# Layer-norm scales asked for by GpSimd, and six chunks instead of five in the seven-product form in the first feed-forward of a tuned decoder trunk

## The chip, the core and the metric

The kernel runs on one core of one Trainium2 chip. Its engines run side by side and are tied together by semaphores: TensorE (PE in the profile, its weight loads PEld), VectorE (DVE), ScalarE (ACT), GpSimd (POOL) and SyncE (SP), which issues transfers. Each engine works through its own list of instructions strictly in order. The metric is device time in microseconds (us).

## The reference: what is computed

Two layers over 256 tokens of width 1024, all in float32. Each layer is a half-step feed-forward, a mixer (forgetting attention in the first layer, latent attention in the second), a second half-step feed-forward and a gated input embedding, each followed by a layer norm:

```python
def swiglu(x, w_in, w_out):
    h = x @ w_in
    gate, up = h[..., :D_FF], h[..., D_FF:]          # D_FF = 2816
    return (jax.nn.silu(gate) * up) @ w_out
...
for i in range(DEPTH):                               # DEPTH = 2
    x = post_norm(x, 0.5 * swiglu(x, ffn1_w_in[i], ffn1_w_out[i]), ln_g[i, 0], ln_b[i, 0])
    mix = fox_mixer(...) if i < N_A else mla_mixer(...)
    x = post_norm(x, mix, ln_g[i, 1], ln_b[i, 1])
    x = post_norm(x, 0.5 * swiglu(x, ffn2_w_in[i], ffn2_w_out[i]), ln_g[i, 2], ln_b[i, 2])
    gate = jax.nn.sigmoid(x @ ple_w_gate[i] + ple_b_gate[i])
    x = post_norm(x, gate * (p[i] @ ple_w_proj[i]), ln_g[i, 3], ln_b[i, 3])
```

`post_norm` is a layer norm of `ALPHA * x + delta` with a scale `g` and a shift `b` of 1024 numbers; there are eight of them.

## The kernel before

**Split products.** Every float32 operand of a matmul is split into a rounded high half and a low half (the rest), and a product is made of three matmuls: high x high, high x low, low x high (`mm3`). Weights come by DMA into one of three buffers `raw` of 1 MB; a unit of 1024 columns is split by an ACT copy (the high half, line 246, or line 254 when it is done ahead) and a DVE subtraction (the low half, line 247 or 258) into one of ten slots `hl` (plus lent tiles such as `gb`, `qk`, `ota`, `otb`). In `mm3` with a weight as the moving operand, the second of the three matmuls is the first to read the weight's low half.

**The feed-forward.** The hidden width of 2816 is cut into eleven chunks of 256. For each chunk, gate and up are 96 matmuls of 256 columns (`HT`), 48 for each half; ACT takes the silu of the gate when the first half is done (line 820), DVE multiplies it with up when the second half is done (line 826). The second product (256 hidden x 1024 out, for two token tiles) is done in one of two ways:

- *plain* (`W`): eight block products of 512 columns, 24 matmuls; two weight units.
- *seven products* (`sums`): a two-by-two block scheme with seven products instead of eight, 21 matmuls. It needs sums of blocks: three DVE additions on the weights (`add` of the stream, lines 294, 300, 302, into the tile `ts` and back into `raw`), three and a half weight units (`ws`, in the order 1, 0, 2, 3; unit 3 is half as wide) and three DVE instructions on the activations (lines 841, 845, 846), after which 896 columns of activations are split (ACT line 623, DVE line 627) into a home tile `fs`, `qk`, `ota` or `otb`.

The seven accumulators stay in PSUM over all such chunks. In the first feed-forward (`cold`) chunk 0 is computed while the first transfers land; chunks 0, 1, 2 and 8, 9, 10 are plain, chunks 3 to 7 use seven products. PE's order there is: chunk 0, then gate and up of chunks 1 to 4, the sums of chunks 3 and 4, gate and up of 5 to 7, the sums of 5 to 7, gate and up of 8 to 10, then the plain products. In the other three feed-forwards chunks 0 to 7 use seven products.

**What sets the order.** While the program is built, a planner (`Stream`) keeps estimated clocks for PE, ACT, DVE and the transfers. After each `mm3` its `pump` may emit one split or one weight addition, if a slot is free and the clocks say that DVE and ACT have caught up with PE. The result is a fixed list for each engine. Weight transfers stand in SP's list in the order of use, and each waits until the `raw` buffer that it overwrites has been split.

**Scale and shift.** `load_gb` asks for the scale and the shift of the next layer norm, 512 KB each when spread over the 128 partitions, into the one tile `gb`, with two requests in SP's list. `gb` has other users: it is lent as a weight slot in the feed-forwards, and holds the attention's decay masks. The request therefore waits until the last of these readers is done. The layer norm itself is four DVE instructions for each token tile at line 702, with a GpSimd power at line 694 ahead of the second; the first at line 702 reads the scale, the second the shift.

Of the kernel before, what the change touches and what calls it, by code (L numbers as in the profile page):

```python
# [11 lines left out]
F32R = mybir.dt.float32r  # L12
# [3 lines left out]
D = 1024  # L16
# [113 lines left out]
class Recorder:  # L130
    def __init__(self):
        self.seq = []
# [12 lines left out]
class Stream:  # L145


    def __init__(self, nc, raw_pool, pool, loads, seq):
        self.nc, self.raw_pool, self.pool, self.loads = nc, raw_pool, pool, loads
        seen = []  # L150
        self.groups = []
        for key in seq:
            g = group_of(key)
            if g not in seen:
                seen.append(g)
                self.groups.append(g)
        members = {g: [] for g in self.groups}
        self.left = {}
        for key in seq:
            if key not in self.left:  # L160
                self.left[key] = 0
                members[group_of(key)].append(key)
            self.left[key] += 1
        self.order = [k for g in self.groups for k in members[g]]
        self.index = {k: i for i, k in enumerate(self.order)}
        self.last_of = {members[g][-1]: i for i, g in enumerate(self.groups)}
        self.raw, self.hl, self.sums, self.added = {}, {}, {}, {}
        self.slots = [f"hl{i}" for i in range(NSLOT)]
        self.slot_of = {}
        self.kept = set()  # L170
        self.loaded = self.ready = 0
        self.done = 0
        self.pending = None
        self.pe_t = self.act_t = self.dve_t = self.dma_t = 0.0
        self.arrives = {}
        self.between = {}
        self.hold = False
        self.rest = None
        self.at = 0
        self.stop = None  # L180
        self.fixed = 80
        self.side = False

    def load(self, n=NRAW):
        while self.loaded < len(self.groups) and self.loaded < self.done + n:
# [81 lines left out]
        self.split_done(key, w)  # L267

    def aside(self, key):
        return self.side and key[0] == "ws" and key[-1] == 3  # L270

    def free(self):
        return self.slots or self.aside(self.order[self.ready])
# [134 lines left out]
def group_of(key):  # L408
    k = key[0]
    if k in ("win", "wiu", "fv", "kd", "dq"):  # L410
        return key[:-1] + (key[-1] // 2,)
    if k == "ws":
        return key[:-1]
    if k in ("wout", "fvb", "fvc", "fk", "fq", "fo", "pg", "pp", "mo", "qr"):
        return key[:-1] + (key[-1] // 2,)
    if k in ("kvk", "qn"):
        return ("kq", key[-1])
    return key
# [81 lines left out]
def pbcast(row, n):  # L500

    return bass.AP(tensor=row.tensor, offset=row.offset, ap=[[0, 128], [1, n]])


class Trunk:
# [162 lines left out]
    def load_gb(self, li, i):  # L668
        first = (li, i) == (0, 0)
        if first:  # L670
            self.tl([128, 16], F32, "gap0", 1)
        self.gb = self.tl([128, 2, D], F32, "gb", 1)
        if first:
            self.tl([128, 16], F32, "gap1", 1)
        if not self.rec:
            self.dma(self.gb[:, 0, :], pbcast(self.a["ln_g"][li, i], D))
            self.dma(self.gb[:, 1, :], pbcast(self.a["ln_b"][li, i], D))

    def ln_stats(self, st, t, c0, w, y, alpha):

# [37 lines left out]
    def ffn(self, li, which, lni, kv=False, ple=False, at=None, cold=False, after=()):  # L718


        nc, S = self.nc, self.S
# [1 line left out]
        g, gT, forms = {}, {}, {}  # L723
        homes = HOMES
        S.reclaim(*(homes if cold else homes[:2]))
        S.fixed, S.side = 150, not cold
        early = (0, 1, 2) if cold else ()
        plain = early + tuple(range(NCH - STAG, NCH))
        summed = [c for c in range(NCH - STAG) if c not in early]

# [5 lines left out]
        def first():  # L736
# [35 lines left out]
            gt = self.room(0, summed)  # L772
            nc.scalar.activation(gt, ps[0], AF.Silu)
            close(0, gt, ps[1])

        def act(c, t, ps):
# [27 lines left out]
        def HT(c, gate, up, what=None):  # L804
            for half in range(2):
                ps = self.bank(*(up if half else gate))
                for u in range(2):
                    w = self.use(("wiu", li, which, c, 2 * half + u))
                    for kk, b in ((kk, b) for kk in range(4) for b in range(2)):
                        k = 4 * u + kk  # L810
                        if (half, k, b) == (0, 1, 0) and what:
                            what(self.bank(*up))
                        col = slice(256 * kk + 128 * b, 256 * kk + 128 * b + 128)
                        self.mm3(
                            ps[:, 256 * b : 256 * b + 256], lambda i: w[:, i, col], lambda i: self.xT[:, :, i, k, :],
                            (k, b) == (0, 0), (k, b) == (7, 1),
                        )
                if half == 0:
                    gt = self.room(c, summed)
                    nc.scalar.activation(gt, ps, AF.Silu)  # L820
                    S.busy(act=512)
            close(c, gt, ps)

        def close(c, gt, up):
            S.ahead()
            nc.vector.tensor_tensor(gt, gt, up, op=ALU.mult)
            self.S.busy(dve=512)
            if c in summed:
                add(c)
                return  # L830
            o = self.tl([128, 2, 512], F32R, "g4", 6)
            self.high(o[:, 0, :], gt)
            S.later()
            self.low(o[:, 0, :], o[:, 1, :], gt)
            gT[c] = o

        def add(c):

            tt, f = nc.vector.tensor_tensor, self.full[c]
            b = lambda i, n=1: f[:, 128 * i : 128 * (i + n)]  # L840
            tt(
                b(4, 2).rearrange("p (a b) -> p a b", b=128), b(0)[:, None, :].to_broadcast([128, 2, 128]),
                b(1, 2).rearrange("p (a b) -> p a b", b=128), op=ALU.subtract,
            )
            tt(b(6), b(5), b(1), op=ALU.subtract)
            tt(b(7), b(6), b(3), op=ALU.add)
            S.busy(dve=700)
            tag, o = self.home(homes)
            self.high(o[:, 0, :], f[:, 128:1024])
            S.between_sums()  # L850
            self.low(o[:, 0, :], o[:, 1, :], f[:, 128:1024])
            forms[c] = tag, o
# [1077 lines left out]
```

## Time and profile before

| | us |
|---|---|
| median of 3 runs | 1055.88 (1055.67 to 1058.72) |
| the profiled execution's own time | 1054.48 |
| its span, first to last instruction | 1052.7 |
| PE busy in the span | 1037.3 (99%) |
| DVE busy | 895.0 (85%) |
| ACT busy | 592.5 (56%) |
| GpSimd busy | 59.9 (6%) |

In a timeline row the numbers are the start (us from the span's start), the time from the first start to the last end of the merged instructions, the engine, the line, the operation, output<-input by tile names, and xcount; in brackets stands the idle time of the engine just before and what ended it. Consecutive instructions overlap a little at their ends, so what an instruction costs in a row of them is the step from start to start. A row of the waits reads: waiting engine and tile <- what ended the wait: total us, times, longest. A row of the windows gives a stretch, its length, and for each engine busy us and instructions.

### The profile page before, as it was taken

The numbers are of one execution on the slowest core, as the hardware profiler recorded it, in microseconds if no ns is written. First come the engines' busy times: TensorE is split into PE (matmuls) and PEld (weight loads), VectorE is DVE, ScalarE is ACT, GpSimd is POOL, SyncE is SP. The second block draws the span as 40 slices with busy tenths as digits, with TensorE's granted clock in tenths as the row PEclk, the third lists the DMA queues.
The fourth block names the chain that finished last, engine by engine and source line by source line (L and its number), as shares of the span: only waits on it lengthen the run. The fifth ranks groups of instructions, "written<-read, shape, count | busy, mean of one in ns | idle before, by whom it ended". The sixth has DMA issues, their size and how long they took to land.

```text
span 1052.7 us, 17554 instructions
## 1 busy us (share of the span) xinstructions
PE 1037.3 (99%) x7085; PEld 949.7 (90%) x7085; DVE 895.0 (85%) x1312; ACT 592.5 (56%) x901; POOL 59.9 (6%) x88
## 2 busy tenths in 40 slices
PE   9999999999999999999899999999999999999996
PEld 8999898999889999998799898988899889898986
DVE  5788976868898979978979899898887989899877
ACT  6565563667745554663465646546776564646541
POOL 0000000123300000000220000000000000000000
PEclk9999999999999999999999999999999999999999
DMA  7855586444736374673564555742444564554732
GB/s 280 307 186 188 194 287 242 161 144 159 257 126 240 120 249 144 219 301 140 190 234 157 201 195 168 277 154 105 151 155 170 184 213 156 184 213 174 279 121 81
DMA packets 37477, 202.74 MB, mean 193 GB/s; under 512 B 3970, under 2 KB 9874, under 8 KB 16532
## 3 DMA queue, kind: packets, MB, share of 16 engines
q1 hardware_dynamic: 37396, 201.63, 54.0%
q8 instruction: 55, 0.90, 0.3%
q14 instruction: 26, 0.21, 0.1%
HBM read 200.55 MB, written 1.06 MB: 192 GB/s over the span
## 4 chain that ended last, share of the span: by engine, by line
PE 68%; DVE 3%; ACT 1%; issue 1%; POOL 0%; DVEq 0%; ACTq 0%; POOLq 0%
PE h L610 37%; PE y L610 21%; PE tr L610 8%; PE tr L614 2%; DVE hl L247 1%; DVE x L702 0%; PE h L614 0%; DVE x L683 0%; DVE st L684 0%; DVE g L1076 0%; ACT hl L246 0%; POOL rs L694 0%; DVE tr L1715 0%; ACT qk L623 0%; ACT P L1340 0%
## 5 line engine op out<-in xcount | busy, mean ns | idle before, releaser
L610 PE MATMUL h<-xT,hl 128*128 128x256 f32 x3144 | 366.9, 278 | 0.2 <-DVE hl L323 0.2
L610 PEld LDWEIGHTS h<-xT,hl 128*128 128x128 f32 x3144 | 362.8, 189 | 2.0 <-ACT xT L623 0.6
L247 DVE TENSOR_TENSOR hl<-raw,hl 128x1024 fp32r<-128x1024 f32 (+4 forms) x273 | 317.3, 1191 | 38.8 <-ACT hl L246 37.6
L246 ACT ACTIVATE hl<-raw 128x1024 fp32r<-128x1024 f32 (+4 forms) x273 | 270.0, 1027 | 72.0 <-DVE raw L302 41.0
L610 PE MATMUL y<-hl,g 128*128 128x512 f32 x336 | 78.6, 391 | 0.0
L610 PEld LDWEIGHTS y<-hl,g 128*128 128x128 f32 x336 | 62.6, 188 | 12.6
L610 PE MATMUL h<-hl,xT 128*128 128x512 f32 (+2 forms) x312 | 68.0, 371 | 0.0
L610 PEld LDWEIGHTS h<-hl,xT 128*128 128x128 f32 x312 | 54.9, 188 | 9.8
L610 PE MATMUL y<-hl,otb 128*128 128x512 f32 x219 | 58.0, 399 | 0.0
L610 PE MATMUL y<-hl,xT 128*128 128x512 f32 (+3 forms) x282 | 52.7, 334 | 0.0
L623 ACT ACTIVATE xT<-tr 128x512 fp32r<-128x512 f32 x28 | 16.3, 597 | 61.7 <-PE tr L614 61.6
L258 DVE TENSOR_TENSOR hl<-raw,hl 128x1024 fp32r<-128x1024 f32 (+2 forms) x42 | 49.7, 1188 | 1.3 <-ACT hl L254 1.2
L254 ACT ACTIVATE hl<-raw 128x1024 fp32r<-128x1024 f32 (+2 forms) x42 | 43.0, 1028 | 9.7 <-DVE raw L302 9.2
L610 PEld LDWEIGHTS y<-hl,xT 128*128 128x128 f32 x282 | 44.1, 188 | 4.6 <-ACT xT L623 0.4
L610 PEld LDWEIGHTS y<-hl,otb 128*128 128x128 f32 x219 | 39.8, 188 | 8.3 <-DVE otb L627 0.3
L610 PE MATMUL y<-hl,ota 128*128 128x512 f32 x177 | 46.7, 398 | 0.1
L694 POOL TENSOR_TENSOR rs<-ve,mhalf 128x1 f32<-128x1 f32 x16 | 15.1, 944 | 522.2 <-DVE ve L693 522.2
L610 PE MATMUL tr<-xT,hl 128*128 128x256 f32 x360 | 42.8, 278 | 0.0
L610 PEld LDWEIGHTS tr<-xT,hl 128*128 128x128 f32 x360 | 42.1, 188 | 0.3
L610 PEld LDWEIGHTS y<-hl,ota 128*128 128x128 f32 x177 | 32.8, 189 | 7.7 <-DVE hl L247 0.6
L820 ACT ACTIVATE P<-h 128x512 f32<-128x512 f32 x33 | 19.7, 596 | 33.2 <-PE h L610 32.8
L294 DVE TENSOR_TENSOR ts<-raw 128x1024 f32<-128x1024 f32 x29 | 35.4, 1222 | 0.6
(324 smaller groups left out, 1638.5 us busy)
## 6 DMA issues: line engine op xcount, KB each, us to landing
raw<-in_ffn_in_dram SPq DMA_DIRECT2D x85, 1024.0 KB, 4.9
raw<-in_ffn_out_dram SPq DMA_DIRECT2D x44, 1024.0 KB, 5.0
raw<-in_pg_dram SPq DMA_DIRECT2D x8, 1024.0 KB, 4.8
raw<-in_mo_dram SPq DMA_DIRECT2D x8, 1024.0 KB, 4.8
raw<-in_kq_dram SPq DMA_DIRECT2D x8, 640.0 KB, 4.2
gb<-in_ln_g_dram SPq DMA_DIRECT2D x8, 512.0 KB, 6.2
gb<-in_ln_b_dram SPq DMA_DIRECT2D x8, 512.0 KB, 7.6
raw<-in_fk_dram SPq DMA_DIRECT2D x4, 1024.0 KB, 5.0
```

The lines of the kernel that those rows point to most:

```text
L246: nc.scalar.activation(hi, src, AF.Copy)
L247: nc.vector.tensor_tensor(lo, src, hi.bitcast(F32), op=ALU.subtract)
L254: nc.scalar.activation(hi, src, AF.Copy)
L258: nc.vector.tensor_tensor(lo, src, hi.bitcast(F32), op=ALU.subtract)
L294: tt(s[:, 0:1024].rearrange("p (a b) -> p a b", b=512), r[:, 0:512][:, None, :].to_broadcast([128, 2, 512]), r[:, 512:1536].rearrange("p ( ...
L610: self.nc.tensor.matmul(out, lhsT, rhs, start=start, stop=stop)
L614: self.nc.tensor.transpose(out, in_, self.ident)
L623: self.nc.scalar.activation(hi, src, AF.Copy)
L694: nc.gpsimd.tensor_tensor(rs, ve, self.mhalf, op=ALU.pow)
L820: nc.scalar.activation(gt, ps, AF.Silu)
```

## The change

1. `load_gb` issues its two requests from GpSimd instead of from SP.
2. In the first feed-forward chunk 2 moves from the plain to the seven-product form: chunks 0, 1, 8, 9, 10 are plain, 2 to 7 use seven products. The sums of chunks 2, 3 and 4 now stand together, ahead of gate and up of chunk 5.
3. There, unit 3 of the weights of chunks 2 to 6 goes into the six-buffer tile `g4` instead of an `hl` slot (`aside`), as it did already in the other feed-forwards for all chunks.
4. The split activations of chunk 0 stay in the tile `PT` instead of a `g4` buffer until the plain products at the end.

```diff
-        self.side = False
+        self.side = ()
...
     def aside(self, key):
-        return self.side and key[0] == "ws" and key[-1] == 3
+        return key[0] == "ws" and key[-1] == 3 and key[-2] in self.side
...
         if not self.rec:
-            self.dma(self.gb[:, 0, :], pbcast(self.a["ln_g"][li, i], D))
-            self.dma(self.gb[:, 1, :], pbcast(self.a["ln_b"][li, i], D))
+            for k, name in enumerate(("ln_g", "ln_b")):
+                self.nc.gpsimd.dma_start(self.gb[:, k, :], pbcast(self.a[name][li, i], D))
...
-        S.fixed, S.side = 150, not cold
-        early = (0, 1, 2) if cold else ()
+        S.fixed, S.side = 150, range(2, 7) if cold else range(8)
+        early = (0, 1) if cold else ()
...
-            o = self.tl([128, 2, 512], F32R, "g4", 6)
+            o = self.tl([128, 2, 512], F32R, "PT", 1) if cold and c == 0 else self.tl([128, 2, 512], F32R, "g4", 6)
```

The planner's lists change with it in the first feed-forward and up to the middle of the first layer's attention; from there on the lists of PE, ACT and DVE are the same but for tile numbers.

DVE at the end of the first sums, before (the activations and weights of chunk 4; `hl7` and `gb` are the first weights of chunk 5's gate):

```order
L627 TENSOR_TENSOR qk_777<-P_708,qk_777 128x896
L247 TENSOR_TENSOR hl5_806<-ts_734,hl5_806 128x1024
L247 TENSOR_TENSOR hl6_815<-ts_734,hl6_815 128x512
L247 TENSOR_TENSOR hl7_823<-raw_604,hl7_823 128x1024
L881 SCALAR_TENSOR_TENSOR x0_69<-x0_69,h0_787 128x512
L247 TENSOR_TENSOR gb_836<-raw_604,gb_836 128x1024
```

DVE at the same place now (`ota_780` the activations of chunk 4, `hl4_809` and `g4_818` the last weights of chunk 3, `raw_607` the weights of chunk 4, `gb_881` the first weight of chunk 5's gate):

```order
L627 TENSOR_TENSOR ota_780<-P_711,ota_780 128x896
L247 TENSOR_TENSOR hl4_809<-ts_737,hl4_809 128x1024
L247 TENSOR_TENSOR g4_818<-ts_737,g4_818 128x512
L294 TENSOR_TENSOR ts_826<-raw_607 128x1024
L300 TENSOR_TENSOR ts_826<-ts_826,raw_607 128x512
L302 TENSOR_TENSOR raw_607<-ts_826,raw_607 128x512
L247 TENSOR_TENSOR hl5_842<-raw_607,hl5_842 128x1024
L247 TENSOR_TENSOR hl6_851<-raw_607,hl6_851 128x1024
L247 TENSOR_TENSOR hl7_860<-ts_826,hl7_860 128x1024
L881 SCALAR_TENSOR_TENSOR x0_69<-x0_69,h0_790 128x512
L247 TENSOR_TENSOR g4_873<-ts_826,g4_873 128x512
L247 TENSOR_TENSOR gb_881<-raw_729,gb_881 128x1024
```

The three weight additions and four low halves of chunk 4 now stand behind those of chunk 3; before, the next gate's weights stood there.

DVE between the two sums, before (`hl4` to `hl7` are the weights of chunk 7's gate and up, `raw_953` the summed weights of chunk 5, `P_1043` the activations of chunk 6):

```order
L247 TENSOR_TENSOR hl6_1034<-raw_906,hl6_1034 128x1024
L247 TENSOR_TENSOR hl7_1052<-raw_906,hl7_1052 128x1024
L294 TENSOR_TENSOR ts_1081<-raw_953 128x1024
L300 TENSOR_TENSOR ts_1081<-ts_1081,raw_953 128x512
L302 TENSOR_TENSOR raw_953<-ts_1081,raw_953 128x512
L247 TENSOR_TENSOR gb_1097<-raw_953,gb_1097 128x1024
L826 TENSOR_TENSOR P_1043<-P_1043,h0_1045 128x512
L841 TENSOR_TENSOR P_1043<-P_1043 128x256
L845 TENSOR_TENSOR P_1043<-P_1043 128x128
L846 TENSOR_TENSOR P_1043<-P_1043 128x128
L258 TENSOR_TENSOR hl8_1106<-raw_953,hl8_1106 128x1024
L627 TENSOR_TENSOR qk_1112<-P_1043,qk_1112 128x896
```

DVE at the same place now (`gb_1118` the last weight of chunk 7's up, `P_1077` the activations of chunk 6, `raw_1022` and `raw_1086` the weights of chunks 5 and 6):

```order
L826 TENSOR_TENSOR P_1077<-P_1077,h0_1079 128x512
L841 TENSOR_TENSOR P_1077<-P_1077 128x256
L845 TENSOR_TENSOR P_1077<-P_1077 128x128
L846 TENSOR_TENSOR P_1077<-P_1077 128x128
L627 TENSOR_TENSOR qk_1145<-P_1077,qk_1145 128x896
L294 TENSOR_TENSOR ts_1167<-raw_1022 128x1024
L300 TENSOR_TENSOR ts_1167<-ts_1167,raw_1022 128x512
L302 TENSOR_TENSOR raw_1022<-ts_1167,raw_1022 128x512
L247 TENSOR_TENSOR hl8_1192<-raw_1022,hl8_1192 128x1024
L247 TENSOR_TENSOR hl9_1210<-raw_1022,hl9_1210 128x1024
L247 TENSOR_TENSOR hl0_1225<-ts_1167,hl0_1225 128x1024
L247 TENSOR_TENSOR g4_1237<-ts_1167,g4_1237 128x512
```

The additions on chunk 5's weights and its first low halves stood ahead of chunk 6's activations, and now stand behind them. Next in the list are the three additions for chunk 6 and line 826 for chunk 7, and then (`P_1204` the activations of chunk 7, `hl1` to `g4` the weights of chunk 6, `raw_1121` the weights of chunk 7, `hl4` the first that its sums read):

```order
L841 TENSOR_TENSOR P_1204<-P_1204 128x256
L845 TENSOR_TENSOR P_1204<-P_1204 128x128
L846 TENSOR_TENSOR P_1204<-P_1204 128x128
L258 TENSOR_TENSOR hl1_1270<-raw_1086,hl1_1270 128x1024
L627 TENSOR_TENSOR ota_1276<-P_1204,ota_1276 128x896
L247 TENSOR_TENSOR hl2_1302<-raw_1086,hl2_1302 128x1024
L247 TENSOR_TENSOR hl3_1311<-ts_1248,hl3_1311 128x1024
L247 TENSOR_TENSOR g4_1320<-ts_1248,g4_1320 128x512
L294 TENSOR_TENSOR ts_1328<-raw_1121 128x1024
L300 TENSOR_TENSOR ts_1328<-ts_1328,raw_1121 128x512
L302 TENSOR_TENSOR raw_1121<-ts_1328,raw_1121 128x512
L247 TENSOR_TENSOR hl4_1338<-raw_1121,hl4_1338 128x1024
```

Before, two low halves of chunk 6 stood ahead of the activations of chunk 7, and now none does.

GpSimd's list from the layer norm behind the first layer's attention to the one behind its input embedding (- before, + now; `hl` at line 250 is the bias row of the embedding's gate):

```order
 L694 TENSOR_TENSOR rs<-ve,mhalf 128x1 x2
-L250 MEMSET hl_5077 128x1024
-L694 TENSOR_TENSOR rs<-ve,mhalf 128x1 x4
+L677 DMA gb<-in_ln_g_dram 128x1024
+L677 DMA gb<-in_ln_b_dram 128x1024
+L250 MEMSET hl_5087 128x1024
+L694 TENSOR_TENSOR rs<-ve,mhalf 128x1 x2
+L677 DMA gb<-in_ln_g_dram 128x1024
+L677 DMA gb<-in_ln_b_dram 128x1024
+L694 TENSOR_TENSOR rs<-ve,mhalf 128x1 x2
 L1444 TENSOR_TENSOR rs<-ve,mhalf 128x1
```

Each pair of requests now stands in GpSimd's list ahead of the powers of the layer norm that it serves, and is gone from SP's, where weight transfers stood behind it.

## The prediction

> **What bounds the kernel now.** I read the page's busy times first, then the waits of PE, then windows over the first feed-forward, where the change moves work.
>
> ```profile
> PE 1037.3 (99%) x7085; PEld 949.7 (90%) x7085; DVE 895.0 (85%) x1312; ACT 592.5 (56%) x901; POOL 59.9 (6%) x88
> PE h L610 <- DVE otb L247: 3.0, 1, 3.0
> PE tr L614 <- DVE x L702: 0.7, 1, 0.7
> 47.00:75.50 28.50, 28.50 (x212) 26.85 (x211) 28.12 (x33) 15.82 (x18) 0.00 (x0) 1.00 0.53 188
> 86.40:131.00 44.60, 44.47 (x328) 41.53 (x328) 43.53 (x52) 24.96 (x29) 0.00 (x0) 1.00 0.52 180
> 130.00:152.00 22.00, 22.00 (x197) 22.00 (x196) 16.18 (x17) 11.95 (x14) 0.00 (x0) 1.00 0.87 305
> ```
>
> PE sets the time: 1037.3 of 1052.7 us, and its longest named wait is 3.0 us. So a change is worth the PE work that it saves, less the waits that it makes. The three windows (length, then PE, PEld, DVE, ACT, POOL, clock) show the catch: from 47 to 75.5 and from 86.4 to 131 DVE is as full as PE, 28.12 of 28.50 and 43.53 of 44.60 us. These are the stretches around the two groups of seven-product sums. What is added to DVE there, or put in another order, reaches PE at once. From 130 to 152 (plain products) DVE idles 5.82 us.
>
> **The PE work saved.**
>
> ```profile
> 66.24 1.52 PE L610 MATMUL y<-hl,qk 128*128 128x512 f32 x6
> 68.28 0.84 PE L610 MATMUL y<-hl,qk 128*128 128x512 f32 x3
> 68.96 0.84 PE L610 MATMUL tr<-hl,qk 128*128 128x512 f32 x3
> 71.00 0.87 PE L610 MATMUL h<-xT,hl 128*128 128x256 f32 x6
> ```
>
> Three matmuls of 512 columns step 68.96 - 68.28 = 0.68 us. A chunk's sums last 71.00 - 66.24 = 4.76 us for 21, eight such threes in the plain form 8 x 0.68 = 5.44. Chunk 2 in the new form saves **0.68 us**, and that is all that this change can save on PE.
>
> **The added DVE work of chunk 2.** It adds three weight additions and one and a half units, and longer activations.
>
> ```profile
> 42.25 2.36 DVE L247 TENSOR_TENSOR hl<-raw,hl 128x1024 fp32r<-128x1024 f32 x2 [0.26 <-ACT hl L246]
> 46.99 1.23 DVE L247 TENSOR_TENSOR gb<-raw,gb 128x1024 fp32r<-128x1024 f32 x1 [2.38 <-ACT gb L246]
> 68.01 1.22 DVE L247 TENSOR_TENSOR hl<-raw,hl 128x1024 fp32r<-128x1024 f32 x1
> 70.88 4.62 DVE L247 TENSOR_TENSOR hl<-raw,hl 128x1024 fp32r<-128x1024 f32 x4
> 83.28 0.42 DVE L841 TENSOR_TENSOR P<-P 128x256 f32<-128x256 f32 x1
> 90.93 1.22 DVE L294 TENSOR_TENSOR ts<-raw 128x1024 f32<-128x1024 f32 x1
> 110.33 1.22 DVE L294 TENSOR_TENSOR ts<-raw 128x1024 f32<-128x1024 f32 x1
> 112.92 2.51 DVE L247 TENSOR_TENSOR hl<-raw,hl 128x1024 fp32r<-128x1024 f32 x2
> ```
>
> The activations (lines 841, 845, 846: about 1.1 us from the row of 0.42 and two half as wide, and a split wider by 0.4) fall into the idle 2.38 us ahead of 46.99: free. If that cover were gone they would cost their 1.5 us. From 46.99 on the list is the old one, one chunk earlier in meaning, up to the last weights of chunk 3, whose half unit ends at 68.01. There chunk 4's additions now stand where the weights of the next gate stood. Three additions last 112.92 - 110.33 = 2.59 us from the first to the first low half, so that low half runs from 70.60 to 70.60 + 1.22 = 71.82. PE comes to chunk 4 at 71.00 and reads the low half with its second matmul, one third of 0.68 later: 71.23. A wait of about **0.6 us** (0.65 with the 0.06 between a DVE end and the PE start behind it). The other low halves follow at 1.14 each against 1.36 for two products, and hold. PE is then 4.76 + 0.65 = 5.41 us late at the next gate; the sums of three chunks stand together, which is that work moved ahead, not added.
>
> **The second sums: where the price lies.** PE does gate and up of chunks 5, 6, 7, then their three sums. DVE must in the same time do the next weights, the additions and the sums' splits, and it has no spare time (the second window). What saved it before was a lead: the additions on chunk 5's weights at 90.93 stood 104.12 - 90.93 = 13.2 us ahead of its sums (row below). In the new list they stand behind line 826 and line 627 of chunk 6, as the third pair of the order lists shows. I follow DVE from A, the end of chunk 6's up on PE.
>
> ```profile
> 77.12 0.60 ACT L820 ACTIVATE P<-h 128x512 f32<-128x512 f32 x1 [4.76 <-PE h L610]
> 82.56 0.69 DVE L826 TENSOR_TENSOR P<-P,h 128x512 f32<-128x512 f32 x1 [1.50 <-PE h L610]
> 85.38 1.09 DVE L627 TENSOR_TENSOR fs<-P,fs 128x896 fp32r<-128x896 f32 x1 [1.02 <-ACT fs L623]
> 104.12 1.54 PE L610 MATMUL y<-gb,fs 128*128 128x512 f32 x6
> 105.77 0.68 DVE L826 TENSOR_TENSOR P<-P,h 128x512 f32<-128x512 f32 x1
> 107.47 1.22 DVE L258 TENSOR_TENSOR hl<-ts,hl 128x1024 fp32r<-128x1024 f32 x1
> 108.61 1.08 DVE L627 TENSOR_TENSOR ota<-P,ota 128x896 fp32r<-128x896 f32 x1
> 109.61 0.68 DVE L247 TENSOR_TENSOR hl<-ts,hl 128x512 fp32r<-128x512 f32 x1
> 113.66 1.97 PE L610 MATMUL y<-hl,ota 128*128 128x512 f32 x6
> 118.95 0.87 PE L610 MATMUL h<-xT,hl 128*128 128x256 f32 x6
> ```
>
> Line 826 cannot run before A: it waits for PE (82.56, 0.20 behind the end of chunk 5's up, as I place it from chunk 7's end at 104.12 less two chunks of 10.88, 96 matmuls at half of 0.2267). Line 627 follows at +2.82 (85.38 - 82.56, with the wait for ACT in it), that is A + 3.02. Steps from the rows: line 627 takes 1.00, a low half 1.14 (107.47 to 108.61), a half-wide one 0.72 (109.61 to 110.33), the additions 2.59, line 826 with 841 to 846 takes 1.70 (105.77 to 107.47). Then
>
> - chunk 5's additions from A + 4.02, first low half A + 6.61, three of these and the half one to A + 10.75;
> - chunk 6's additions to A + 13.34, chunk 7's line 826 and the next three to A + 15.04;
> - one low half of chunk 6 to A + 16.18, line 627 of chunk 7 to A + 17.18, two low halves and the half one to A + 20.18;
> - chunk 7's additions to A + 22.77, its first low half ends at A + 23.99.
>
> PE wants that low half at A + 10.88 (gate and up of 7) + 9.54 (113.66 - 104.12, two chunks of sums) + 0.23 = A + 20.65. With the 0.06 it waits **3.4 us** in all, in pieces at chunks 6 and 7, since A + 16.18 is already late for chunk 6 by about half a us. Before, the same third chunk took 118.95 - 113.66 = 5.29 instead of 4.76, a loss of 0.53 that goes with it.
>
> What bounds this term: below, 0.5 us, if DVE arrives at the sums as it does now; above, 3.4 plus one low half of 1.14 if ACT's high halves, which stand in its list behind line 820 (77.12, idle 4.76 for PE), come late once more. I take 3.4, since the list fixes the order and each step is a row of this stretch. What is late next: the plain weights of chunks 8 to 10 and the removed chunk 2; there the third window has DVE idle by a quarter, and the two units of chunk 2 are gone. So PE loses nothing more.
>
> **The requests on GpSimd.**
>
> ```profile
> SPq L541 <- DVE x L702: 46.5, 5, 22.4
> ACT hl L246 <- DMA raw<-in_ffn_in_dram: 7.5, 7, 2.8
> 492.77 0.33 SPq L541 DMA_DIRECT2D gb<-in_ln_g_dram  x1
> gb<-in_ln_g_dram SPq DMA_DIRECT2D x1, 512.0 KB, 3.6
> gb<-in_ln_b_dram SPq DMA_DIRECT2D x1, 512.0 KB, 9.4
> 504.58 0.75 DVE L702 SCALAR_TENSOR_TENSOR x<-x,rs,gb 128x512 f32<-128x512 f32 x1 [0.45 <-POOL rs L694]
> 506.93 0.63 PE L614 MATMUL tr<-ident,x 128*128 128x128 f32 x4 [0.71 <-DVE x L702]
> 521.65 2.03 POOL L1459 TENSOR_SCALAR PT<-PT,rs 128x256 f32<-128x256 f32 x1
> 1028.57 0.33 SPq L541 DMA_DIRECT2D gb<-in_ln_g_dram  x1
> 1038.07 0.75 DVE L702 SCALAR_TENSOR_TENSOR x<-x,rs,gb 128x512 f32<-128x512 f32 x1 [0.44 <-POOL rs L694]
> ```
>
> SP is freed of five waits, 46.5 us in all. I price this at nothing: the one larger wait for the weights of a feed-forward is ACT's 7.5 us in seven pieces, and ACT is busy 56% and splits ahead of PE, which has no wait of its own behind it. What it costs if GpSimd is slower: each request waits for the same last reader as before, so it cannot go out earlier. The trace has no transfer asked for by GpSimd; a request lies between SP's 0.33 us and the slowest GpSimd row, 2.03; I take the nearer, SP's. Two layer norms are close: behind the first input embedding the pair goes out from 492.77 and the shift is read at 504.58; at the end 1028.57 against 1038.07. Landings go from 3.6 us (the window at 492) to 9.4 (a layer norm at 987). At SP's price both hold: 0.
>
> **Sum.** -0.68 + 0.65 + 3.42 - 0.53 = **+2.9 us** on the profiled 1054.48, or 1057.35. The median of the runs lies 1055.88 - 1054.48 = 1.40 above it, so 1057.35 + 1.40 = **1058.8 us**. Items 3 and 4 of the change give slots and take no instruction away: nothing, beyond what the lists above already hold.
>
> **Rivals.** *DVE keeps up.* If the additions for chunk 5 start as far ahead as now, only -0.68 + 0.65 stays: 1055.9, and 1055.2 without either wait. For it: DVE stood idle 1.50 and 1.02 us in this stretch before (82.56, 85.38), which a late PE could fill. Against it: the list puts the additions behind line 826 of chunk 6, and that cannot move. *SP's freedom pays.* If the 3.0 us wait for `otb` at 517.8 hung on a late transfer behind the requests, it would go: 1058.8 - 3.0 = 1055.8, with the first rival 1052.2. Against it:
>
> ```profile
> 514.77 1.04 ACT L246 ACTIVATE otb<-raw 128x1024 fp32r<-128x1024 f32 x1
> 519.93 1.22 DVE L247 TENSOR_TENSOR otb<-raw,otb 128x1024 fp32r<-128x1024 f32 x1
> ```
>
> ACT had split the high half by 515.8, so the data were there; the low half stands behind DVE's layer norm, whose order does not change. *The scale and shift land late (slower).* With 2.03 us for each of two requests and 9.4 to land, the shift is there at 492.77 + 4.06 + 9.4 = 506.2, 1.6 after it is read, and PE's transposes wait directly (506.93); at the end 1028.57 + 13.46 = 1042.0, 4.0 late. With the sum above that is 1058.8 + 1.6 + 4.0 = 1064.4. It decides once request and landing together exceed 11.8 us at 492.7 or 9.5 at 1028.5. For it: 9.4 was seen in the trace; against: at the first of these places the scale took 3.6.
>
> [...]
>
> **Chances.** The forecast 0.57, DVE keeping up 0.18, SP's freedom 0.08, late landing 0.15, another 0.02. A measurement can tell about 0.3%, 3.2 us: faster is below 1052.7, slower above 1059.05. The forecast's own spread, 1057.4 to 1060.2 by the bounds above, passes the upper one in nearly half of its cases: 0.26 slower, 0.31 same. Late landing adds 0.13 slower and 0.02 same; DVE keeping up and the other 0.20 same; SP's freedom 0.05 faster (with the first rival), 0.03 same. So 0.05, 0.56 and 0.39. The range 1055.0 to 1060.8 holds the forecast, the first rival, and SP's freedom without it.
>
> **What would show it.** Right: between 100 and 125 us PE waits on DVE low halves at line 247 or 258, about 3 us; a wait of 0.6 near 71; GpSimd's requests with no new wait at line 702. Wrong: no wait at the second sums and DVE idle ahead of them; the wait at 517.8 gone; or DVE at line 702 ended by a transfer into `gb` near 504 or 1038.

## The result and the profile after

The changed kernel took 1059.43 us (median of 14 runs, 1058.06 to 1063.73), the kernel before, in 14 runs beside it, 1056.33. The ratio is **1.0031**, 95% interval 1.0020 to 1.0043: slower by 3.3 us, between 2.1 and 4.5. The forecast was +2.9 us. The profiled execution took 1058.98 us (span 1057.2), 4.5 more than that of before.

PE's waits now, then PE around the second sums (rows of the timeline):

```profile
PE h L610 <- DVE otb L247: 3.0, 1, 3.0
PE y L610 <- DVE hl L247: 1.9, 1, 1.9
PE y L586 <- POOL mhalf L571: 1.2, 1, 1.2
...
PE h L610 <- DVE hl L247: 0.5, 1, 0.5
...
PE y L610 <- DVE hl L258: 0.4, 1, 0.4
```

```profile
110.13 1.54 PE L610 MATMUL y<-hl,fs 128*128 128x512 f32 x6
...
114.91 0.39 PE L610 MATMUL y<-hl,qk 128*128 128x512 f32 x1
115.66 1.43 PE L610 MATMUL y<-hl,qk 128*128 128x512 f32 x5 [0.36 <-DVE hl L258]
116.92 0.40 PE L610 MATMUL h<-hl,qk 128*128 128x512 f32 x1
117.80 0.73 PE L610 MATMUL h<-hl,qk 128*128 128x512 f32 x2 [0.47 <-DVE hl L247]
...
121.09 0.40 PE L610 MATMUL y<-hl,ota 128*128 128x512 f32 x1
123.38 1.43 PE L610 MATMUL y<-hl,ota 128*128 128x512 f32 x5 [1.89 <-DVE hl L247]
...
128.15 0.85 PE L610 MATMUL h<-xT,gb 128*128 128x256 f32 x6
```

Three stops, 0.36, 0.47 and 1.89 us, where before lost half a us. Each comes one matmul into a new weight unit, right ahead of the first matmul that reads its low half, and DVE's work on that low half (line 258 or 247) ends it. The three sums last 128.15 - 110.13 = 18.02 us, against 118.95 - 104.12 = 14.83 before. DVE in the same stretch:

```profile
99.45 0.69 DVE L826 TENSOR_TENSOR P<-P,h 128x512 f32<-128x512 f32 x1 [0.36 <-PE h L610]
...
102.28 1.09 DVE L627 TENSOR_TENSOR qk<-P,qk 128x896 fp32r<-128x896 f32 x1 [1.02 <-ACT qk L623]
103.28 1.22 DVE L294 TENSOR_TENSOR ts<-raw 128x1024 f32<-128x1024 f32 x1
...
110.08 1.23 DVE L294 TENSOR_TENSOR ts<-raw 128x1024 f32<-128x1024 f32 x1
...
114.39 1.22 DVE L258 TENSOR_TENSOR hl<-raw,hl 128x1024 fp32r<-128x1024 f32 x1
...
119.51 1.22 DVE L294 TENSOR_TENSOR ts<-raw 128x1024 f32<-128x1024 f32 x1
...
122.11 2.49 DVE L247 TENSOR_TENSOR hl<-raw,hl 128x1024 fp32r<-128x1024 f32 x2
```

With A at 99.45 - 0.20 = 99.25, the prediction's chain reads: line 627 at A + 3.03 (worked out: 3.02), the three additions at A + 4.03, 10.83 and 20.26 (4.02, 10.75, 20.18), chunk 7's first low half from A + 22.86 (22.77). Nothing on DVE stands still between 103 and 123.

**Where the 4.5 us of the two profiles come from.** At the first row of line 702, the first layer norm, the changed kernel is 3.74 us behind:

```profile
182.92 0.74 DVE L702 SCALAR_TENSOR_TENSOR x<-x,mv,gb 128x512 f32<-128x512 f32 x1
```

Before:

```profile
179.18 0.74 DVE L702 SCALAR_TENSOR_TENSOR x<-x,mv,gb 128x512 f32<-128x512 f32 x1
```

The second sums give 18.02 - 14.83 = +3.19. The first sums last 77.02 - 62.38 = 14.64 for three chunks against 9.53 for two (71.00 - 61.47); with 4.77 for the one chunk more taken off, +0.34. The saved PE work is -0.68. That makes 2.85, and the rest, 0.9, was there before the sums began: PE reaches them at 62.38 instead of 61.47, with the same work and 0.2 us of named waits. PE up to and behind the first sums, in the profile after:

```profile
56.73 2.99 PE L610 MATMUL h<-xT,gb 128*128 128x256 f32 x24
59.56 2.99 PE L610 MATMUL h<-xT,hl 128*128 128x256 f32 x24
62.38 1.55 PE L610 MATMUL y<-hl,fs 128*128 128x512 f32 x6
...
77.02 0.86 PE L610 MATMUL h<-xT,gb 128*128 128x256 f32 x6
```

And before (its first sums end at 71.00):

```profile
56.03 2.88 PE L610 MATMUL h<-xT,gb 128*128 128x256 f32 x24
58.75 2.88 PE L610 MATMUL h<-xT,hl 128*128 128x256 f32 x24
61.47 1.54 PE L610 MATMUL y<-hl,fs 128*128 128x512 f32 x6
```

Twenty-four matmuls of 256 columns step 2.83 us in the profile after (56.73 to 59.56), where before had 2.72 (56.03 to 58.75). This is taken up below. From the layer norm on, the distance grows once more, by 1.7 us between 517 and 692 us, where the granted clock fell (windows; the column behind the busy times is the clock):

```profile
525.00:530.00 5.00, 5.00 (x15) 3.96 (x16) 4.46 (x5) 2.28 (x3) 4.82 (x5) 0.66 0.84 290
```

(5 - 0.66 x 5 = 1.7.) In the profile of before the clock was 1.00 there. Behind 692 us 0.9 of this distance is lost again (5.42 us there, 4.56 at the last layer norm's end, about 1046), half of it at the end, where this time the matmuls of before have the slower pace (2.95 us for 25 of 256 columns against 2.83). So of the 4.5 us, 2.85 are the change nearly as predicted (2.9), and the rest, +0.9, +1.7 and -0.9, belongs to these two executions.

GpSimd's requests behind the first input embedding, and what they took to land:

```profile
496.75 0.57 POOL L677 DMA_DIRECT2D gb<-in_ln_g_dram  x1 [2.53 <-DVE x L702]
497.32 0.54 POOL L677 DMA_DIRECT2D gb<-in_ln_b_dram  x1
gb<-in_ln_b_dram POOLq DMA_DIRECT2D x1, 512.0 KB, 5.1
508.26 0.75 DVE L702 SCALAR_TENSOR_TENSOR x<-x,rs,gb 128x512 f32<-128x512 f32 x1 [0.46 <-POOL rs L694]
```

The shift lands at 497.32 + 5.1 = 502.4 and is read at 508.26. At the end the pair has less room:

```profile
1034.52 0.53 POOL L677 DMA_DIRECT2D gb<-in_ln_b_dram  x1
gb<-in_ln_b_dram POOLq DMA_DIRECT2D x1, 512.0 KB, 5.2
1043.06 0.75 DVE L702 SCALAR_TENSOR_TENSOR x<-x,rs,gb 128x512 f32<-128x512 f32 x1 [0.46 <-POOL rs L694]
```

It lands at 1039.7 and is read at 1043.06. Over all eight layer norms the median landing is 6.5 us for the scale and 7.2 for the shift, against 6.2 and 7.6 on SP. DVE's waits at line 702 are those of before, 0.4 to 0.5 us each and none ended by a transfer.

### The profile page after: what moved, and what is told of

It reads as the page before. It is cut to its first block, busy times and chain, and to the rows that moved or that the text cites. A ratio compares the mean times of both kernels' runs of the same rounds, so it can differ in the third digit from the quotient of the medians.

```text
span 1057.2 us, 17565 instructions
## 1 busy us (share of the span) xinstructions
PE 1038.8 (98%) x7082; PEld 951.0 (90%) x7082; DVE 900.4 (85%) x1320; ACT 594.8 (56%) x903; POOL 68.4 (6%) x104
## 4 chain that ended last, share of the span: by engine, by line
PE 68%; DVE 3%; ACT 1%; issue 1%; POOL 0%; DVEq 0%; ACTq 0%; POOLq 0%
PE h L610 37%; PE y L610 21%; PE tr L610 8%; PE tr L614 2%; DVE hl L247 1%; DVE x L702 0%; PE h L614 0%; DVE x L683 0%; DVE st L684 0%; DVE g L1076 0%; ACT hl L246 0%; POOL rs L694 0%; DVE tr L1715 0%; ACT qk L623 0%; ACT P L1340 0%
## 5 line engine op out<-in xcount | busy, mean ns | idle before, releaser
L247 DVE TENSOR_TENSOR hl<-raw,hl 128x1024 fp32r<-128x1024 f32 (+3 forms) x272 | 316.4, 1191 | 41.8 <-ACT hl L246 40.6
L246 ACT ACTIVATE hl<-raw 128x1024 fp32r<-128x1024 f32 (+3 forms) x272 | 269.1, 1027 | 62.7 <-DVE raw L302 39.5
L610 PE MATMUL y<-hl,g 128*128 128x512 f32 x312 | 73.5, 392 | 0.0
L610 PEld LDWEIGHTS y<-hl,g 128*128 128x128 f32 x312 | 57.9, 188 | 11.5
L610 PE MATMUL y<-hl,ota 128*128 128x512 f32 x189 | 50.2, 398 | 1.9 <-DVE hl L247 1.9
L610 PE MATMUL y<-hl,xT 128*128 128x512 f32 (+3 forms) x264 | 50.1, 336 | 0.0
L610 PEld LDWEIGHTS y<-hl,xT 128*128 128x128 f32 x264 | 41.4, 188 | 4.5 <-ACT xT L623 0.4
L677 POOL DMA_DIRECT2D gb<-in_ln_g_dram x8 | 4.8, 606 | 571.0 <-PE y L610 238.1
```

Of the source, the lines that this page charges most:

```text
L246: nc.scalar.activation(hi, src, AF.Copy)
L247: nc.vector.tensor_tensor(lo, src, hi.bitcast(F32), op=ALU.subtract)
L610: self.nc.tensor.matmul(out, lhsT, rhs, start=start, stop=stop)
L677: self.nc.gpsimd.dma_start(self.gb[:, k, :], pbcast(self.a[name][li, i], D))
```

## The experiments

The runs, each against the kernel before on the same chip:

| run | chunks | requests | else | ratio, interval |
|---|---|---|---|---|
| first | five | GpSimd | | 0.9999 (0.9986 to 1.0013) |
| second | six | SP | | 1.0037 (1.0023 to 1.0052) |
| third | six | SP | early additions | 1.0018 (1.0005 to 1.0031) |
| fourth | five | SP | the same planner number | 0.9997 (0.9987 to 1.0008) |
| fifth | six | GpSimd | early additions | 1.0004 (0.9993 to 1.0014) |
| sixth | six | SP | early additions, `otb` split earlier | 0.9969 (0.9956 to 0.9981) |
| seventh | five | SP | the same two | 0.9964 (0.9949 to 0.9980) |
| eighth | six | SP | one addition three times | 1.0055 (1.0039 to 1.0071) |
| ninth | five | SP | items 3 and 4 | 1.0005 (0.9994 to 1.0016) |
| tenth | six | SP | without item 3 | 1.0043 (1.0027 to 1.0059) |
| eleventh | five | SP | `otb` split earlier | 0.9965 (0.9951 to 0.9978) |

**The requests alone.** The kernel before with this:

```diff
-            self.dma(self.gb[:, 0, :], pbcast(self.a["ln_g"][li, i], D))
-            self.dma(self.gb[:, 1, :], pbcast(self.a["ln_b"][li, i], D))
+            for k, name in enumerate(("ln_g", "ln_b")):
+                self.nc.gpsimd.dma_start(self.gb[:, k, :], pbcast(self.a[name][li, i], D))
```

> The kernel before with nothing changed but the sixteen requests for scale and shift, which GpSimd makes now. My account (they are worth nothing): the same time as before within 0.1%, no new wait at line 702, and the 3.0 us wait for otb near 517.8 stays. Rival one (a late landing): 1.6 us longer at the input embedding of the first layer and up to 4 us at the end, with line 702 ended by the transfer into gb. Rival two (SP's freedom pays): 3 us faster, the wait near 517.8 gone.

Measured 1055.40 against 1055.64 us, ratio 0.9999. The wait for `otb` stays (3.0 us in its waits too). Worth nothing, and both rivals fall: neither a landing nor SP's freedom reaches PE.

**Six chunks with the requests on SP.** The changed kernel with that hunk taken back.

> The changed kernel with the requests back on SP: six chunks, side slots and chunk 0 in PT alone. My account: all of the 3.3 us (+0.3%) stays, with the three waits of PE near 115, 117 and 121 us that add up to about 3 us. Rival (the requests on GpSimd cost the time): as fast as before.

Measured 1059.58 us, ratio 1.0037: all of the loss. PE stops at the second sums for 0.4, 0.5 and 1.87 us. At the first sums it stops for 0.6 us; in the changed kernel's own profile, where it came to these sums later (from 20 to 60 us its windows of five us hold 357 matmuls, those of the second run 371), it hardly stopped there (0.2 us). And behind the longest stop PE slows down:

```profile
122.10 2.47 PE L610 MATMUL y<-hl,ota 128*128 128x512 f32 x5 [1.87 <-DVE hl L247]
124.37 1.42 PE L610 MATMUL h<-hl,ota 128*128 128x512 f32 x3
125.63 0.86 PE L610 MATMUL y<-hl,ota 128*128 128x512 f32 x3
120.00:125.00 5.00, 3.13 (x8) 2.32 (x8) 4.38 (x5) 3.47 (x4) 0.00 (x0) 0.72 0.28 74
```

The five matmuls at 122.10 take 2.27 us to the next row and the three at 124.37 take 1.26, where the changed kernel's profile had 1.27 (123.38 to 124.65) and 0.70: 1.6 us more, and the clock stands at 0.72 over these five us.

**The lead given back.** Six chunks, SP, and one number of the planner:

```diff
-        S.fixed, S.side = 150, range(2, 7) if cold else range(8)
+        S.fixed, S.side = (80 if cold else 150), range(2, 7) if cold else range(8)
```

> Six chunks with the requests on SP, and one number of the planner changed in the first feed-forward: it counts 80 ns instead of 150 for each DVE instruction, and so puts the additions on chunk 5's weights and one of their low halves ahead of chunk 6's activations again. The work of every engine is the same. My account (the lost lead makes the waits): the waits at the second sums shrink from 3.0 us to about 0.6, the time is 2.5 to 4 us below the changed kernel, at or just under the kernel before. Rival (DVE has not enough time for the work of three chunks, in whatever order): the waits keep their sum of 3 us and only move, time as of the changed kernel.

The waits went as my account had it. PE at chunk 7's sums, and DVE ahead of them:

```profile
119.36 1.96 PE L610 MATMUL y<-hl,ota 128*128 128x512 f32 x6
121.15 0.85 PE L610 MATMUL h<-hl,ota 128*128 128x512 f32 x3
```

```profile
99.22 1.22 DVE L247 TENSOR_TENSOR hl<-raw,hl 128x1024 fp32r<-128x1024 f32 x1
100.36 0.68 DVE L826 TENSOR_TENSOR P<-P,h 128x512 f32<-128x512 f32 x1
```

The first two products take 1.79 us (119.36 to 121.15) instead of 1.36 or so: 0.4 us is lost, and the list of waits has none on `hl` at line 247 any more. Chunk 5's additions and one of its low halves stand ahead of line 826 again. The rival that DVE lacks the time, whatever the order, falls: the work is the same. The time went from 1.0037 to 1.0018, less than I had put it: the expected 2.5 to 4 us became 2.3 between the medians (1059.58 and 1057.26), and the kernel stayed 1.6 us above the one before (1055.64).

**The same number with five chunks.**

```diff
-        S.fixed, S.side = 150, not cold
+        S.fixed, S.side = (80 if cold else 150), not cold
```

> The kernel before with the same planner number, five chunks. It tells how much of the run before this one belongs to the number and not to the six chunks. If the sixth chunk is worth its 0.68 us once the lead is kept, this kernel is 0.5 to 1 us slower than six chunks with early additions, and within 1 us of the kernel before.

Ratio 0.9997. The number alone is worth nothing with five chunks, and five were faster than six here, 1054.91 against 1057.26 us, where I had expected the reverse by 0.5 to 1.

**Again, with GpSimd's requests.** The changed kernel with the planner's number.

> The changed kernel as it is (six chunks, requests on GpSimd) with the planner's 80 ns for 150 in the first feed-forward: the third run with the requests on GpSimd instead of SP. My account: the requests are worth nothing, so the time is that of the third run (1.0018 of before) within its interval; the waits at the second sums stay gone. If the third run's 1.8 us over the kernel before was chance (the slow early pace of PE in its profile), this one lies at or below the kernel before; if six chunks cost something that the waits do not show, it lies 1 to 3 us above it again.

Ratio 1.0004. The long stop stays gone (the list of PE's waits in its profile has none on `hl` at line 247). The likeliest reading is that the third run's 1.0018 was high by chance, as the intervals allow (they meet between 1.0005 and 1.0014); it is not shown, since the two runs differ in the requests too. Six chunks with the lead kept show no loss that stands in both runs, and no gain either.

**The wait for `otb`.** Six chunks, and five, each with the planner's number and one split moved ahead of a layer norm:

```diff
             for c0, c1 in full:
                 post(1, c0, c1)
+            S.split()
             self.ln_apply(1, st[1][0][:, 0:2, :], LN_EPS)
```

> Six chunks with the early additions, requests on SP, and one weight split moved in the list: the unit in otb that follows the input embedding of the first layer is split ahead of the last layer norm's line 702 instead of behind it. PE waited 3.0 us for it in every profile, and in all but the first the granted clock fell to 0.66 for 5 us right behind. Account one (the clock falls because PE stands still): the wait near 518 falls to under 1 us, the clock stays at 1.00 there, 3 to 5 us faster than the third run. Account two (the clock falls by itself, whatever PE does): only 2 to 3 us faster, with 0.66 still in a window near 520.

> The same moved split with five chunks and the planner's 80 ns: 3 to 5 us faster than the fourth run by the first account of the clock, 2 to 3 by the second. Against the run with six chunks it tells what the sixth chunk is worth on undisturbed ground: 0.7 us in favour of six if only PE's work counts, against it if the third run's loss was real.

Ratios 0.9969 and 0.9964: 1052.93 and 1052.34 us, both faster than both kernels. From the third and fourth run that is 4.3 and 2.6 us by the medians, the second less than the 3 to 5 that I had put for the account that the clock falls because PE stands still. In the sixth run's profile the clock is 1.00 from 515 to 530. The sixth chunk's 0.7 us cannot be seen on this ground either. The intervals hide a difference of that size, and the six chunks still wait for DVE at their first sums. PE there in the sixth run:

```profile
71.18 1.43 PE L610 MATMUL y<-hl,ota 128*128 128x512 f32 x5 [0.67 <-DVE hl L247]
```

That stop is as long as the saved work.

**The wait for `otb` alone.** The kernel before with the same one line.

> The kernel before with one thing moved: the split of the unit in otb stands ahead of the last layer norm's line 702 behind the first input embedding. If the gain of the seventh run lies in the wait and the clock behind it, all of it is here: 3 to 4 us faster than before, no window near 520 with a clock under 1.00.

Ratio 0.9965, 1053.02 against 1056.29 us, 3.3 us faster. DVE, PE and the clock of this kernel:

```profile
516.00 1.21 DVE L247 TENSOR_TENSOR otb<-raw,otb 128x1024 fp32r<-128x1024 f32 x1
517.12 0.20 DVE L692 BATCH_NORM_AGGREGATE mv<-st 128x2 f32<-128x12 f32 x1
```

```profile
517.65 1.55 PE L610 MATMUL h<-otb,xT 128*128 128x512 f32 x6
519.04 1.08 PE L610 MATMUL h<-hl,xT 128*128 128x512 f32 x4
520.62 2.14 PE L610 MATMUL h<-hl,xT 128*128 128x512 f32 x8 [0.50 <-ACT hl L246]
```

```profile
520.00:530.00 10.00, 9.45 (x53) 7.97 (x53) 8.79 (x13) 6.29 (x9) 6.59 (x8) 1.00 0.67 255
```

The low half runs at 516.00 instead of 519.93, PE goes on at 517.65, and of the 3.0 us a wait of 0.5 is left.

**A longer stop.** The second run's kernel with the first addition for chunk 7 done three times (the same values again):

```diff
+            for _ in range(3 if g == ("ws", 0, "ffn1", 7) else 1):
                 tt(
                     s[:, 0:1024].rearrange("p (a b) -> p a b", b=512), ...
```

> The kernel of the second run (six chunks, requests on SP, old planner number) with the first addition on chunk 7's weights done three times, the same values each time: 2.5 us more of DVE ahead of the last of the three sums, no other change. My account (DVE's list decides when PE has that weight): the wait near 120 us grows from 1.9 to 4.4 us and the time by 2.5 us, and by up to 1.5 more where the granted clock falls behind the longer stop. Rival (PE waits there for something else, a transfer or ACT): the wait and the time stay as in the second run.

```profile
118.50 3.74 DVE L295 TENSOR_TENSOR ts<-raw 128x1024 f32<-128x1024 f32 x3
...
123.61 2.49 DVE L247 TENSOR_TENSOR hl<-raw,hl 128x1024 fp32r<-128x1024 f32 x2
```

```profile
124.89 1.50 PE L611 MATMUL y<-hl,ota 128*128 128x512 f32 x4 [4.37 <-DVE hl L247]
```

(One line was added, so lines behind it count one more.) The stop grew from 1.87 to 4.37 us, 2.50 more, one for one; the median is 1062.19 us, 2.6 above the second run's. So DVE's list sets when PE has that weight, and not a transfer or ACT.

**Items 3 and 4.** The kernel before with unit 3 of chunks 3 to 6 in `g4` and chunk 0's activations in `PT`; and six chunks without item 3:

```diff
-        S.fixed, S.side = 150, not cold
+        S.fixed, S.side = 150, range(3, 7) if cold else range(8)
```

```diff
-        S.fixed, S.side = 150, range(2, 7) if cold else range(8)
+        S.fixed, S.side = 150, () if cold else range(8)
```

> Five chunks, requests on SP, and items 3 and 4 of the change alone: unit 3 of the weights of chunks 3 to 6 in g4, chunk 0's activations in PT. My account: nothing, the order of the lists is that of before and only the tiles' names differ; the time is that of before within 0.15%.

> The second run's kernel (six chunks, requests on SP) without item 3: unit 3 of the weights goes into an hl slot. My account: the slots never set the time here, so the three waits at the second sums stay (3 us) and so does the loss of 0.3 to 0.4%. Rival (the waits come from where unit 3 lies): the waits change by more than half a us in sum.

Ratios 1.0005 and 1.0043. In the tenth run's profile PE's longest waits on `hl` at line 247 are 1.9 and 0.5 us, as in the changed kernel (1.89 and 0.47). Where unit 3 lies decides nothing here.

## Why the prediction was right

**The bound.** PE is 98% busy in the changed kernel too. What was added to DVE in its two full stretches reached PE as predicted; the eighth run shows one of them one for one.

**The saved work**, 0.68 us: one block product less. No run isolates it: with the lead kept, six chunks and five came out alike (0.9969 and 0.9964), and in the sixth run a stop of 0.67 us at the first sums stands against it.

**The first sums**, +0.65: measured +0.34 in the profile after and a stop of 0.6 us in the second run. The mechanism was right, the size depends on when PE comes: in the profile after it began chunk 4's sums at 71.95 instead of the predicted 71.00, and DVE's low half, begun at 70.99 instead of 70.60, was nearly ready.

**The second sums**, +3.42 - 0.53 = +2.89: measured +3.19. The list walked by row durations held to 0.1 us over 23 us. Of the remaining 0.3, 0.24 lies on PE's side: the 20 matmuls behind the last stop took 4.77 us (123.38 to 128.15) where 20 steps of 0.227 are 4.53. The two sums together came to 3.53 us where 3.54 was forecast; that the misses, -0.31 and +0.30, cancel is luck, and so is part of the closeness of 2.9 to 3.3. The range within which I expected the forecast, 1057.4 to 1060.2, does not come out of the bounds either: 0.5 and 3.4 plus 1.14 give 1055.9 to 1060.0. And I gave the same time more chance than a slower one, 0.56 against 0.39, because I held 3.2 us for the least that can be told; the interval of 2.1 to 4.5 us is finer than that.

**The requests**, 0: shown by the first run. A request took 0.57 us, near the 0.33 that I took and far from 2.03. Two readings behind that zero were wrong. I took SP's five waits for `x` of line 702, 46.5 us, as those of these requests. Line 541 is the helper of other requests too, and in the changed kernel three of the waits remain:

```profile
SPq L541 <- DVE x L702: 40.5, 3, 32.7
```

And the requests could go out earlier: the third pair went at 429.56 us instead of 451.28, because in SP's list it had stood behind weight transfers that waited for their buffers (16.8 us in four waits at line 471 between 425 and 455). Neither reached PE, since DVE did not wait for the scale or the shift in either kernel. GpSimd's landings took about as long as SP's: medians of 6.5 and 7.2 us against 6.2 and 7.6.

**Items 3 and 4**, 0: shown by the ninth and tenth run.

**The rivals.** DVE keeping up: fell, by the three stops. SP's freedom: fell, the `otb` wait is 3.0 us with the requests on either engine; its cause was the place of one DVE instruction, as the eleventh run shows. Late landing: fell, by 3.3 us at the end and 5.8 behind the first input embedding.

**What it lacked.** Two things that differ between executions of one list. The clock fell behind some stops of PE, and such a stop cost more than its length: 1.87 us of stop cost 1.6 more in the second run's profile, with a clock of 0.72 from 120 to 125. And PE's early pace differs between executions by 4% (2.72 and 2.83 us for 24 matmuls). Over many runs the mean granted clock was 0.9948 for the changed kernel and 0.9966 for the kernel before (30 runs beside the first four; 0.9959 and 0.9962 in the two later sets of 19), so part of the 3.3 us may be clock; how much, the runs do not separate, since their interval (2.1 to 4.5) holds the forecast without it. The other kernels that keep the long stop have as low a clock (second run 0.9953, eighth 0.9948, tenth 0.9950), and six chunks without it do not (third 0.9963, fifth 0.9966).

## What to carry to other kernels

When the order of work is fixed ahead, walk the list of the engine that feeds the bound, with durations from neighbouring rows, from the last event that it cannot pass; here that foretold 3 us of waits that no share of busy time shows. A saving of work on the bound engine can be worth less than the lead that its feeder had: 0.68 us was bought for 3.5. And look at the longest single wait of the bound engine first: here one split moved ahead of a layer norm was worth 3.3 us, as much as the whole change cost.

## What the runs showed of the hardware

**The granted clock fell behind some short stops of PE.** With the 3.0 us stop for `otb`, the ten us from 520 to 530 had a mean clock of 0.83 in the profiles of the changed kernel and of the second, third and fourth run, 0.66 in that of the first, and 1.00 in that of before; with the stop gone, 1.00 in the sixth run's (515 to 530) and in the eleventh's (520 to 530). Behind the stop of 1.9 us at the second sums it fell in one of three profiles (0.72 from 120 to 125 in the second run's; 1.00 in the changed kernel's and the tenth run's), behind that of 4.37 us in its one profile (0.66 from 125 to 130). So it fell once behind a stop of 1.87 us, and once it did not behind one of 3.0. Over whole executions the mean clock agrees: 0.9980, 0.9977 and 0.9975 in the three kernels without the stop for `otb` (6, 7 and 8 runs), 0.9948 to 0.9968 in all others. Where the clock fell, the matmuls stepped slower: in the second run's profile eight of 512 columns take 3.53 us (122.10 to 125.63), 0.44 each, and the next three 0.70, 0.23 each. The seventeen behind `otb` take 5.62 us in the changed kernel's profile (524.89 to 530.51) and 4.02 in that of before (521.20 to 525.22).

**Two paces of the same matmuls.** Twenty-four matmuls of 256 columns take 2.72 or 2.83 us, for many groups in a row, with the granted clock at 1.00 in both. In some profiles PE runs at the faster pace from 30 us on at the latest (before, second, fourth, sixth to eighth and tenth run: 46 or 47 matmuls in each window of five us from 30 to 60), in others at the slower (44 or 45) until the first sums or even the second (changed kernel, first, third, fifth, ninth and eleventh). The first and ninth have the order of before, so it is not the order. The fifth and the sixth run have the same order up to the first sums; from 20 to 60 us the windows of five us hold 358 matmuls in the one profile and 370 in the other, so the pace costs some 1.4 us there, an estimate from these counts (12 matmuls at 2.83 / 24). It can also come back: in the last input embedding before takes 2.95 us for 25 such matmuls (1036.99 to 1039.94), after 2.83 (1041.82 to 1044.65). What starts and ends it stays open.
